# Two rings for the second plain tile of the output projections

## The chip, the cores and the metric

The kernel runs on one core of a Trainium2 chip. The metric is the device time of one execution in microseconds; the median of three runs of the kernel before is 1833.44 us. Several engines work side by side and each takes its own instructions in a fixed order: PE (TensorE, matrix products), DVE (VectorE), ACT (ScalarE), POOL (GpSimd, here mostly an issuer of transfers) and SP (SyncE, the issuer of all weight loads).

## The reference, cut to what matters

One step of a two-layer encoder over 640 tokens (512 of a prompt, 128 samples) with 2048 channels. The last step of each layer is the output projection, and only this step is touched:

```
y_a = c * silu(a_gate)                     # convolution group
y_b = o_b * silu(b_gate)                   # window attention group
y_c = mem_attention(cq, mem_k, mem_v) * silu(c_gate)
y = concatenate([y_a, y_b, y_c], axis=-1) @ w_out
return x + y, new_conv, new_k, new_v
```

## The kernel before, in words

Activations stand with channels on partitions: `R` holds 16 tiles of 128 channels by 640 tokens. A float32 product is made of three products of a high and a low half: each operand is split into a rounded copy (`split`, an ACT copy on L138) and the remainder (a DVE subtraction on L139). `HL` holds the split activations, high halves first. A weight tile of 128 output channels comes as four parts of 128x512; each part is loaded by SP (L149), split by ACT and DVE, and read by 24 products of 128x320 on PE (four blocks of 128 rows, three passes, two halves of the tokens).

Two sets of buffers hold such weights. The ring of the input projection lies in the pool `wp`: `wr` for the load, `wh` and `wl` for the halves, three buffers each; `wprep` uses it. The ring of the output projection lies in the pool `sw`: `sr` (six buffers for loads), `sh` and `sl` (two each); `s_prep` uses it. `sr` tiles may have 768 columns.

An output projection (from L1069 on) has 16 output tiles. Tiles j=0 and j=1 are "plain": 96 products each, L760, with the sum going to a `z` tile of PSUM; L1115 then adds the residual (`zt`) and writes `R`. The other tiles go in pairs through `s_pair`, a seven-product scheme of the Strassen kind on the middle and last channels: `combos` first makes differences of tiles of `R` (L789, eight per layer, some in place) and splits them into `th`/`tl` (three combinations, two pieces each) and back into `HL` (one combination, two pieces). `th`/`tl` live in the pool `tt`, which is opened on the same side of memory as `wp`, after `wp` is closed: of the three combinations the third (`th4`, `tl4`) lies over `wh` and `wl`, the first `tl` over `wr`. A tile waits for the last reader of what lies under it.

The first pair begins with a product `X` (18 products, weights `p1`, first loads of the pair), then `plain(True)`: 18 products with the part `a12` as loaded, then 18 with `a12 - s2` (a DVE subtraction of 128x768, L789, followed by its own split). The difference `s2` comes from `s1 = a21 + a22` (L843), which needs the third load of the pair's four.

In layer 1, L1074 first stores six tiles of `R` to memory (`y12d`, 960 KB, by POOL); the in-place differences of `combos` wait until it has landed.

The order within an engine is set by a scheduler when the program is built, from the order in the code and from priorities; weight loads and splits are of high priority. `sh_8724` and the like are names with their buffer number.

Of the kernel before, what the change touches and what calls it, by code (L numbers as in the profile page):

```python
# [58 lines left out]
def build(nc, tc, ctx, A):  # L59
# [15 lines left out]
    def open_pool(n, side):  # L75
        uid[0] += 1
        held_pools[n] = tc.tile_pool(name=f"{n}{uid[0]}", bufs=1, reuse_waits="tile", side=side)
        cur[n] = held_pools[n].__enter__()

    def close_pool(n):  # L80
        held_pools.pop(n).__exit__(None, None, None)
# [9 lines left out]
    def zt():  # L91
        return tl([P, TOK], "zt", 2)
# [16 lines left out]
    def pz():  # L109
        return tl([P, 2, 512], "z", 2, F32, zp)  # L110
# [22 lines left out]
    def half(t):  # L133
        return t.rearrange("p (s n) -> p s n", s=2)
# [114 lines left out]
    def add_sq(k, first, acc, tmp=w25):  # L249
        if first:  # L250
            ac.activation(acc, R[:, k, :], AF.Square)
        else:
            sq = tmp()
            ac.activation(sq, R[:, k, :], AF.Square)
            ve.tensor_tensor(out=acc, in0=acc, in1=sq, op=ALU.add)
# [495 lines left out]
    def proj(wsrc, prep=wprep):  # L751
        ps = pz()
        for pc in range(4):
            wh, wl = prep(wsrc[pc])
            for kk in range(4):
                k = pc * 4 + kk
                ws = slice(kk * P, (kk + 1) * P)
                for n, (w, lo) in enumerate(((wh, 0), (wh, 1), (wl, 0))):
                    for s in range(2):
                        pe.matmul(  # L760
                            ps[:, s, :HT], w[:, ws], HL[:, lo * NK + k, s * HT:(s + 1) * HT],
                            start=k == 0 and n == 0, stop=k == NK - 1 and n == 2,
                        )
        return ps
# [29 lines left out]
    def combos():  # L794
        T = {}
        tt = [
            (tl([P, 6, HT], f"th{n}", 1, F32R, cur["tt"]), tl([P, 6, HT], f"tl{n}", 1, F32R, cur["tt"]))
            for n in (2, 3, 4)
        ]
        T[2], T[3], T[4] = tt  # L800
        T[1] = hl(KA, TB)
        gs = [(slice(KA.start + g, KA.start + g + 3), slice(KB.start + g, KB.start + g + 3)) for g in (0, 3)]
        for a, b in gs:
            sub(R[:, a, TA], R[:, a, TB], R[:, a, TA])
            sub(R[:, a, TB], R[:, b, TB], R[:, a, TB])
            sub(R[:, b, TB], R[:, b, TB], R[:, a, TA])
        place = {1: (0, TA), 2: (1, TB), 3: (0, TB), 4: (1, TA)}
        for n in (3, 2, 4, 1):
            for g, ab in enumerate(gs):
                i, cs = place[n]  # L810
                if n == 4:
                    sub(R[:, ab[1], TA], R[:, ab[1], TA], R[:, ab[1], TB])
                ks = slice(3 * g, 3 * g + 3)
                split(R[:, ab[i], cs], None, T[n][0][:, ks, :], T[n][1][:, ks, :])
        return T
# [90 lines left out]
    for l in range(L):  # L906
# [35 lines left out]
        for n, (kind, i) in enumerate(ZT):  # L942
            if l == 0 and n in (8, 9):
                o, i_ = (("o_kold", "ck"), ("o_vold", "cv"))[n - 8]
                with tc.issue_after(late):
                    gp.dma_start(A[o], A[i_][:, :, ST:, :])
            ps = proj(A["w_in"][l, n])
            if n == 0:
                rstd_row(rstd, acc, 1.0 / D)
# [158 lines left out]
        for j in list(range(2)) + list(range(2, done, 2)):  # L1108
            if j < 2:
                res = zt()  # L1110
                gp.dma_start(res, resid[j])
                ps = proj(
                    [A["w_out"][l, j][:, c * 512:(c + 1) * 512] for c in range(4)], s_prep if j else wprep
                )
                ve.tensor_tensor(out=half(R[:, j, :]), in0=ps[:, :, :HT], in1=half(res), op=ALU.add)  # L1115
            else:
                s_pair(l, j, T, resid, turn if j + 2 == done else None)
            if j == 0:
                close_pool("wp")
                open_pool("tt", "right")  # L1120
            if j == 1:
                T = combos()
            for i in range(j, j + 1 if j < 2 else j + 2):
                if l == 0:
                    gp.dma_start(x1d[i], R[:, i, :])
                add_sq(i, i == 0, acc)
# [173 lines left out]
```

## Time and profile before

| what | value |
|---|---|
| runs | 1833.44, 1833.44, 1834.79 us |
| the profiled execution's own time | 1833.57 us |
| its span, first to last instruction | 1831.8 us |
| PE busy (12580 products) | 1803.6 us, 98% of the span |
| DVE, ACT, POOL busy | 1258.1, 785.0, 174.0 us |
| mean granted PE clock | 0.996 |
| output projection of layer 0, plain tiles | from about 739 to 774 us |
| output projection of layer 1, plain tiles | from about 1591 to 1628 us |

The span is 1.8 us shorter than the execution's own time; both are of the same execution. PE is busy nearly throughout, so time is to be looked for where PE stood still: in the views of waits and in the timeline around the two places in the table. In a row of the timeline the first number is the start in us from the span's start, the second how long the merged instructions took, then engine, line, operation, tiles, their number, and in brackets the idle time of the engine before it with what ended it.

### The profile page before, as it was taken

The page shows a single profiled execution, that of the slowest core. Times are in us where ns is not written, and L with a number is a line of the kernel's source. Part 1 is how long each engine was busy: PE and PEld are TensorE (multiplying, and loading weights), DVE is VectorE, ACT ScalarE, POOL GpSimd, SP SyncE. Part 2 cuts the span into 40 slices and gives each one's busy share as a digit, 9 for nine tenths or more (in the row PEclk, how much of TensorE's full clock was granted, in tenths as well). Part 3 has the DMA queues.
Part 4 walks back from the last instruction along what each step waited for, and adds up shares of the span by engine and source line. Part 5 has one row for each costly group of instructions (what it writes and reads, how often), then busy time and mean ns, then how long its engine had stood idle before and what let it go on. Part 6 is the DMA issues. An engine that isn't in the chain of part 4 may idle for free.

```text
span 1831.8 us, 32312 instructions
## 1 busy us (share of the span) xinstructions
PE 1803.6 (98%) x12580; PEld 1766.5 (96%) x12580; DVE 1258.1 (69%) x2562; ACT 785.0 (43%) x1593; POOL 174.0 (9%) x383
## 2 busy tenths in 40 slices
PE   8999999999999999999999999999999999999996
PEld 7899999999999999999999999999999999989996
DVE  7959999567555445966686999766655544776765
ACT  7831224556644334533352222555755333533331
POOL 1121210000001010100030010000001110010000
PEclk9999999999999999999999999999999999999998
DMA  8844442222222343533333332222222244442233
GB/s 283 290 129 103 105 130 76 70 64 70 87 78 84 98 162 116 171 134 116 109 102 89 82 81 78 78 67 73 73 84 85 74 139 132 158 160 84 71 113 121
DMA packets 89193, 202.30 MB, mean 110 GB/s; under 512 B 12064, under 2 KB 17104, under 8 KB 89008
## 3 DMA queue, kind: packets, MB, share of 16 engines
q1 hardware_dynamic: 68848, 139.75, 25.3%
q0 software_dynamic: 17728, 57.60, 10.3%
q10 hardware_dynamic: 2464, 2.88, 0.5%
q8 instruction: 99, 1.62, 0.4%
q14 instruction: 54, 0.44, 0.1%
HBM read 184.84 MB, written 20.33 MB: 112 GB/s over the span
## 4 chain that ended last, share of the span: by engine, by line
PE 94%; DVE 3%; DMA 2%; issue 1%; ACT 0%; SPq 0%; DVEq 0%; ACTq 0%; POOLq 0%
PE z L760 59%; PE a L821 9%; PE z L821 9%; PE a L278 2%; PE z L301 2%; PE a L497 2%; PE a L540 2%; PE a L477 2%; PE z L1145 1%; DVE R L1178 1%; PE a L528 1%; DMA wr<-w_in 1%; PE a L647 1%; PE a L673 1%; PE a L686 1%
## 5 line engine op out<-in xcount | busy, mean ns | idle before, releaser
L760 PE MATMUL z<-HL,wh 128*128 128x320 f32 x4992 | 979.5, 312 | 0.0
L760 PEld LDWEIGHTS z<-HL,wh 128*128 128x128 f32 x4992 | 788.9, 188 | 7.9 <-issue 5.3
L760 PE MATMUL z<-HL,wl 128*128 128x320 f32 x2496 | 580.4, 311 | 0.7 <-DVE wl L139 0.7
L760 PEld LDWEIGHTS z<-HL,wl 128*128 128x128 f32 x2496 | 419.3, 188 | 2.0 <-DVE wl L139 1.0
L138 ACT ACTIVATE wh<-wr 128x512 fp32r<-128x512 f32 x316 | 198.7, 629 | 448.6 <-PE z L760 373.1
L139 DVE TENSOR_TENSOR wl<-wr,wh 128x512 fp32r<-128x512 f32 x316 | 218.0, 690 | 172.7 <-ACT wh L138 163.6
L425 DVE SCALAR_TENSOR_TENSOR R<-R,sm 128x128 f32<-128x128 f32 (+1 forms) x480 | 235.4, 552 | 0.1
L138 ACT ACTIVATE sh<-sr 128x768 fp32r<-128x768 f32 (+1 forms) x125 | 98.3, 787 | 206.2 <-PE a L821 91.4
L821 PE MATMUL z<-HL,sh 128*128 128x320 f32 x728 | 160.9, 309 | 1.9 <-ACT sh L138 1.9
L139 DVE TENSOR_TENSOR sl<-sr,sh 128x768 fp32r<-128x768 f32 (+1 forms) x125 | 110.1, 881 | 40.7 <-ACT sh L138 40.5
L821 PEld LDWEIGHTS z<-HL,sh 128*128 128x128 f32 x728 | 121.7, 188 | 2.4 <-ACT sh L138 2.4
L821 PE MATMUL z<-HL,sl 128*128 128x320 f32 x364 | 113.4, 312 | 0.9 <-DVE sl L139 0.7
L139 DVE TENSOR_TENSOR g<-a,g 128x512 fp32r<-128x512 f32 x80 | 49.5, 634 | 39.8 <-ACT g L138 39.2
L821 PE MATMUL a<-th,sh 128*128 128x320 f32 x234 | 72.2, 308 | 0.0
L821 PE MATMUL a<-tl,sh 128*128 128x320 f32 x234 | 72.2, 308 | 0.0
L821 PE MATMUL a<-th,sl 128*128 128x320 f32 x234 | 72.2, 308 | 0.0
L821 PEld LDWEIGHTS z<-HL,sl 128*128 128x128 f32 x364 | 68.3, 188 | 3.2 <-DVE sl L139 3.2
L821 PE MATMUL a<-HL,sh 128*128 128x320 f32 x312 | 68.9, 308 | 0.0
L138 ACT ACTIVATE g<-a 128x512 fp32r<-128x512 f32 x80 | 42.1, 551 | 53.1 <-PE a L531 29.9
L501 DVE CUSTOM_DVE_ANT_0 g<-a,R 128x256 f32<-128x256 f32 (+1 forms) x128 | 46.4, 388 | 23.4 <-PE a L497 20.0
L513 ACT ACTIVATE g<-g,sml 128x256 f32<-128x256 f32 (+1 forms) x128 | 59.8, 468 | 0.0
L485 POOL DMA_DIRECT2D R<-brep x32 | 17.3, 541 | 407.3 <-issue 238.2
(263 smaller groups left out, 2536.0 us busy)
## 6 DMA issues: line engine op xcount, KB each, us to landing
wr<-w_in SPq DMA_DIRECT2D x304, 256.0 KB, 2.7
sr<-w_out SPq DMA_DIRECT2D x52, 384.0 KB, 3.3
sr<-w_out SPq DMA_DIRECT2D x34, 256.0 KB, 2.6
u<-w_mv SPq DMA_DIRECT2D x16, 512.0 KB, 4.0
u<-cmkT POOLq DMA_DIRECT2D x16, 512.0 KB, 3.6
u<-cmv POOLq DMA_DIRECT2D x16, 512.0 KB, 4.3
u<-w_mk SPq DMA_DIRECT2D x14, 512.0 KB, 5.1
R<-xT SPq DMA_DIRECT2D x16, 320.0 KB, 4.7
```

What stands on the lines that cost most here:

```text
L138: a = ac.activation(hi, raw, AF.Copy)
L139: v = ve.tensor_tensor(out=lo, in0=raw, in1=hi.bitcast(F32), op=ALU.subtract)
L278: pe.matmul(ps[ct][:, :256], w[:, ws], mslot(l, k, lo), start=k == 0 and n == 0, stop=k == NK - 1 and n == 2,)
L301: pe.matmul(psv[:, m, :], mslot(l, k, lo)[:, ms], w, start=k == 0 and n == 0, stop=k == NK - 1 and n == 2,)
L425: ve.scalar_tensor_tensor(out=o, in0=x, scalar=w, in1=o, op0=ALU.mult, op1=ALU.add)
L477: pe.matmul(ps[:, :HT], w[:, ws], x[:, k, :], start=n == 0, stop=n == 11)
L497: pe.matmul(ps[:, j, c0:256], q[:, p * P:(p + 1) * P], kk[n][h][:, (p - 1) * P + c0:(p + 1) * P], start=n == 0, stop=n == 1,)
L501: ve.tensor_tensor_reduce(out=x[:, j, c0:], in0=ps[:, j, c0:], in1=bt[:, c0:], scale=1.0, scalar=-3.0e38, op0=ALU.add, op1=ALU.max, accum_ ...
L513: ac.activation(x, x, AF.Exp, bias=ng[:, p:p + 1], accum_out=sm_[:, p:p + 1])
L540: pe.matmul(po[:, os], V[h][:, v, :], p[:, ms], start=v == 0 and n == 0, stop=v == 3 and n == 1, skip_group_check=True,)
L760: pe.matmul(ps[:, s, :HT], w[:, ws], HL[:, lo * NK + k, s * HT:(s + 1) * HT], start=k == 0 and n == 0, stop=k == NK - 1 and n == 2,)
L821: pe.matmul(out, a[:, k * P:(k + 1) * P], b[:, k, :], start=start and k == 0 and i == 0, stop=stop and k == n - 1 and i == 2, skip_group_c ...
```

## The change

In both layers the second plain tile (j=1) takes the first two of its four weight parts through the input projection's ring (`wprep`) and the last two through the output projection's (`s_prep`); before, all four went through the latter. `wp` is therefore closed, and `tt` opened in its place, after tile j=1 and no longer after tile j=0.

```
     def proj(wsrc, prep=wprep):
         ps = pz()
         for pc in range(4):
-            wh, wl = prep(wsrc[pc])
+            wh, wl = (prep[pc] if isinstance(prep, list) else prep)(wsrc[pc])
...
                 ps = proj(
-                    [A["w_out"][l, j][:, c * 512:(c + 1) * 512] for c in range(4)], s_prep if j else wprep
+                    [A["w_out"][l, j][:, c * 512:(c + 1) * 512] for c in range(4)], [wprep, wprep, s_prep, s_prep] if j else wprep
                 )
...
-            if j == 0:
+            if j == 1:
                 close_pool("wp")
                 open_pool("tt", "right")
-            if j == 1:
                 T = combos()
```

How this moves instructions shows best on DVE. In layer 0, around the residual sum of tile 0 (`L1115 ... z_8530`), this stood before; `sl_8724` and `sl_8754` are the low halves of the third and fourth weight part of tile 1, `tl` are the combinations:

```order
L1115 TENSOR_TENSOR R<-z_8530,zt_8528 128x640
L789 TENSOR_TENSOR R<-R 128x3x320
L139 TENSOR_TENSOR tl_1362_8785<-R,th_1361_8784 128x960 x2
L139 TENSOR_TENSOR tl_1360_8783<-R,th_1359_8782 128x960
L139 TENSOR_TENSOR tl_1364_8787<-R,th_1363_8786 128x960
L139 TENSOR_TENSOR tl_1360_8783<-R,th_1359_8782 128x960
L139 TENSOR_TENSOR sl_8724<-sr_8721,sh_8723 128x512
L139 TENSOR_TENSOR tl_1364_8787<-R,th_1363_8786 128x960
L139 TENSOR_TENSOR sl_8754<-sr_8751,sh_8753 128x512
L843 TENSOR_TENSOR sr_8832<-sr_8822,sr_8824 128x768
```

And this stands there now, up to the residual sum; `wl_8660` and `wl_8690` are the first and second part of tile 1, `sl_8720` and `sl_8750` the third and fourth:

```order
L139 TENSOR_TENSOR wl_8660<-wr_8657,wh_8659 128x512
L789 TENSOR_TENSOR R<-R 128x3x320
L139 TENSOR_TENSOR sl_8720<-sr_8717,sh_8719 128x512
L139 TENSOR_TENSOR sl_8750<-sr_8747,sh_8749 128x512
L139 TENSOR_TENSOR HL<-R,HL 128x640
L139 TENSOR_TENSOR wl_8690<-wr_8687,wh_8689 128x512
L843 TENSOR_TENSOR sr_8832<-sr_8822,sr_8824 128x768
L789 TENSOR_TENSOR R<-R 128x3x320
L789 TENSOR_TENSOR sr_8833<-sr_8832,sr_8820 128x768
L789 TENSOR_TENSOR sr_8822<-sr_8820,sr_8822 128x768
L789 TENSOR_TENSOR R<-R 128x3x320
L1115 TENSOR_TENSOR R<-z_8530,zt_8528 128x640
```

All four splits of tile 1's weights and the three operations on the pair's weights now stand ahead of the residual sum; two differences and all six `tl` follow it in one piece.

A little later on DVE, from the first split of the pair (`sl_8829`, weights of `X`) to that of the subtracted part (`sl_8881`), this stood before in layer 0 (`sr_8826` is `a12`, `w` the running sum of squares, `z_8660` the sum of tile 1):

```order
L139 TENSOR_TENSOR sl_8829<-sr_8820,sh_8828 128x768
L139 TENSOR_TENSOR HL<-R,HL 128x3x320
L1115 TENSOR_TENSOR R<-z_8660,zt_8658 128x640
L139 TENSOR_TENSOR sl_8858<-sr_8826,sh_8857 128x768
L139 TENSOR_TENSOR HL<-R,HL 128x3x320
L789 TENSOR_TENSOR sr_8826<-sr_8826,sr_8833 128x768
L255 TENSOR_TENSOR w_1329_8527<-w_1329_8527,w_1365_8813 128x640
L827 TENSOR_TENSOR R<-a_8818,R 128x320
L139 TENSOR_TENSOR sl_8881<-sr_8826,sh_8880 128x768
```

and this stands there now, in layer 0 and with other numbers in layer 1:

```order
L139 TENSOR_TENSOR sl_8829<-sr_8820,sh_8828 128x768
L1115 TENSOR_TENSOR R<-z_8656,zt_8654 128x640
L139 TENSOR_TENSOR HL<-R,HL 128x3x320
L139 TENSOR_TENSOR sl_8858<-sr_8826,sh_8857 128x768
L139 TENSOR_TENSOR HL<-R,HL 128x3x320
L255 TENSOR_TENSOR w_1329_8527<-w_1329_8527,w_1365_8813 128x640
L827 TENSOR_TENSOR R<-a_8818,R 128x320
L789 TENSOR_TENSOR sr_8826<-sr_8826,sr_8833 128x768
L139 TENSOR_TENSOR sl_8881<-sr_8826,sh_8880 128x768
```

The residual sum of tile 1 has moved ahead of a split into `HL`, and the subtraction from `a12` has moved behind L255 and L827. In layer 1 the subtraction stood behind these two before as well.

SP's queue (layer 0) now has `wr_8657`, `wr_8687`, `sr_8717`, `sr_8747` where it had `sr_8661`, `sr_8691`, `sr_8721`, `sr_8751`, then the pair's four loads as before. The first row below is the last load of tile 0:

```order
L149 DMA wr_8621<-w_out 128x512
L149 DMA wr_8657<-w_out 128x512
L149 DMA wr_8687<-w_out 128x512
L149 DMA sr_8717<-w_out 128x512
L149 DMA sr_8747<-w_out 128x512
L149 DMA sr_8820<-w_out 128x768
L149 DMA sr_8822<-w_out 128x768
L149 DMA sr_8824<-w_out 128x768
L149 DMA sr_8826<-w_out 128x768
```

The two `wr` loads wait for buffers of a ring of three that tile 0 still uses, and the six `sr` loads are issued behind them.

More of the change, by code (lines that the diff above doesn't have):

```diff
@@ L753, in proj @@
         for pc in range(4):
-            wh, wl = prep(wsrc[pc])
+            wh, wl = (prep[pc] if isinstance(prep, list) else prep)(wsrc[pc])
             for kk in range(4):
@@ L1112, in build @@
                 ps = proj(
-                    [A["w_out"][l, j][:, c * 512:(c + 1) * 512] for c in range(4)], s_prep if j else wprep
+                    [A["w_out"][l, j][:, c * 512:(c + 1) * 512] for c in range(4)], [wprep, wprep, s_prep, s_prep] if j else wprep
                 )
@@ L1117, in build @@
                 s_pair(l, j, T, resid, turn if j + 2 == done else None)
-            if j == 0:
+            if j == 1:
                 close_pool("wp")
                 open_pool("tt", "right")
-            if j == 1:
                 T = combos()
```

## The prediction

> **What bounds the kernel now.** I read the page first, then PE's waits in the two stretches where the plain tiles of the output projection run, then the timeline there, and last the transfers.
>
> ```profile
> span 1831.8 us, 32312 instructions
> PE 1803.6 (98%) x12580; PEld 1766.5 (96%) x12580; DVE 1258.1 (69%) x2562; ACT 785.0 (43%) x1593; POOL 174.0 (9%) x383
> PE 94%; DVE 3%; DMA 2%; issue 1%; ACT 0%; SPq 0%; DVEq 0%; ACTq 0%; POOLq 0%
> ```
>
> PE is busy for 98% of the span and the chain that ended last is PE for 94%. The change leaves the number and size of the products alone, so it can only move time at which PE stands still near the plain tiles. These are PE's waits there, first all of layer 0 (720 to 800 us), then all of layer 1 (1580 to 1660 us); the three numbers are the total, the times, the longest:
>
> ```profile
> PE z L760 <- DVE sl L139: 1.4, 1, 1.4
> ...
> PE z L760 <- DVE sl L139: 2.3, 1, 2.3
> PE z L821 <- ACT sh L138: 1.4, 1, 1.4
> PE z L821 <- DVE sl L139: 0.7, 2, 0.4
> ```
>
> Each layer loses once inside a plain tile (L760, a low weight half that came late), and layer 1 loses again in the first pair (L821). Together this is some 6 us; no way of ordering this stretch can win more than that, 0.3% of the time. The timeline shows the first loss, in layer 0 and in layer 1:
>
> ```profile
> 761.53 5.42 DVE L139 TENSOR_TENSOR tl<-R,th 128x960 fp32r<-128x960 f32 x5
> 765.51 0.75 PE L760 MATMUL z<-HL,sh 128*128 128x320 f32 x4
> 766.87 0.68 DVE L139 TENSOR_TENSOR sl<-sr,sh 128x512 fp32r<-128x512 f32 x1
> 767.61 0.57 PE L760 MATMUL z<-HL,sl 128*128 128x320 f32 x2 [1.35 <-DVE sl L139]
> ...
> 1618.23 0.75 PE L760 MATMUL z<-HL,sh 128*128 128x320 f32 x4
> 1621.31 0.56 PE L760 MATMUL z<-HL,sl 128*128 128x320 f32 x2 [2.33 <-DVE sl L139]
> ```
>
> Five splits of the combinations (`tl`) hold DVE for 5.4 us, and the split of tile 1's third weight part stands behind them. PE has done its four products with the high half and waits.
>
> The second place is what I call the tail: from PE's first product of the pair (`a<-HL,sh`) to the first low product with the subtracted part (`z<-HL,sl`), 38 products later. First layer 0, then layer 1:
>
> ```profile
> 773.30 0.75 PE L760 MATMUL z<-HL,sh 128*128 128x320 f32 x4
> 774.09 0.85 ACT L138 ACTIVATE sh<-sr 128x768 fp32r<-128x768 f32 x1 [1.34 <-PE z L760]
> 774.18 0.46 PE L821 MATMUL a<-HL,sh 128*128 128x320 f32 x2
> 774.38 0.82 DVE L1115 TENSOR_TENSOR R<-z,zt 128x640 f32<-128x640 f32 x1 [0.44 <-PE z L760]
> ...
> 780.07 0.41 PE L821 MATMUL z<-HL,sl 128*128 128x320 f32 x1
> ...
> 1627.87 0.46 PE L821 MATMUL a<-HL,sh 128*128 128x320 f32 x2
> 1629.52 0.82 DVE L1115 TENSOR_TENSOR R<-z,zt 128x640 f32<-128x640 f32 x1
> 1630.25 0.95 DVE L139 TENSOR_TENSOR sl<-sr,sh 128x768 fp32r<-128x768 f32 x1
> 1631.12 1.16 DVE L139 TENSOR_TENSOR HL<-R,HL 128x960 fp32r<-128x960 f32 x1
> 1632.19 0.49 DVE L827 TENSOR_TENSOR R<-a,R 128x320 f32<-128x320 f32 x1
> 1632.59 0.82 DVE L255 TENSOR_TENSOR w<-w,w 128x640 f32<-128x640 f32 x1
> 1633.32 0.96 DVE L789 TENSOR_TENSOR sr<-sr,sr 128x768 f32<-128x768 f32 x1
> 1634.39 1.36 ACT L138 ACTIVATE sh<-sr 128x768 fp32r<-128x768 f32 x2 [3.28 <-DVE sr L789]
> 1635.27 1.56 DVE L139 TENSOR_TENSOR sl<-sr,sh 128x768 fp32r<-128x768 f32 x2 [0.99 <-ACT sh L138]
> 1636.28 0.42 PE L821 MATMUL z<-HL,sl 128*128 128x320 f32 x1 [0.43 <-DVE sl L139]
> ```
>
> From 773.30 to 774.18 six products start, so one takes 0.147 us, and 38 take 5.57 us. The tail took 5.89 us in layer 0 and 8.41 us in layer 1, where the subtraction (L789) stood behind L827 and L255.
>
> **The change part by part.** *Equal work.* Four loads, eight split instructions and 96 products per tile stay, and the 256 KB of each load; cost 0.
>
> *First loss.* All four splits of tile 1 now stand ahead of the `tl`, so no `tl` can hold them up. The losses by starts are 767.61 - 765.51 - 4 x 0.147 = 1.51 us and 1621.31 - 1618.23 - 4 x 0.147 = 2.49 us. I take both away: -4.00 us.
>
> *Tail.* Late next is the tail. The new DVE order is the residual sum (L1115), a split into `HL`, a weight split, a split into `HL`, L255, L827, the subtraction. L1115 waits for tile 1's last product: it starts 0.20 us after the pair's first product (774.38 - 774.18). From the starts in layer 1's rows: L1115 0.73, `HL` 1.07, weight split 0.87, `HL` 1.07, L255 0.73, L827 0.40, together 4.87; subtraction to ACT's copy 1.07, copy to DVE's split 0.88, split to PE 1.01. Sum 0.20 + 4.87 + 2.96 = 8.03 us, against 5.57 us of products: the cover is gone in layer 0. The tail grows by 8.03 - 5.89 = 2.14 us there; layer 0 is left at -1.51 + 2.14 = +0.63 us. A PE wait inside the tail (the first two products of `plain` now stand ahead of the low products of `X` and wait for an ACT copy) is no extra: DVE sets the end.
>
> *Layer 1's DVE.* The same tail holds only if DVE has finished what stands ahead of L1115 of tile 1. That begins with the split of tile 1's second part, held by the ring: its high half can be copied when PE has read the third part of tile 0.
>
> ```profile
> L138 ACT ACTIVATE wh<-wr 128x512 fp32r<-128x512 f32 x316 | 198.7, 629 | 448.6 <-PE z L760 373.1
> ...
> 1601.59 0.69 DVE L139 TENSOR_TENSOR wl<-wr,wh 128x512 fp32r<-128x512 f32 x1
> ...
> 1611.63 0.46 PE L760 MATMUL z<-HL,wl 128*128 128x320 f32 x2
> ...
> 1617.36 2.22 DVE L139 TENSOR_TENSOR tl<-R,th 128x960 fp32r<-128x960 f32 x2
> ```
>
> Tile 0's last product started at 1611.63 + 0.15 = 1611.78; five products of tile 1 no longer stand ahead of it (-0.73), and the last reader of the buffer lies 26 products earlier (-3.82): 1607.23. ACT copies 0.35 us after such a reader (774.09, the last of the four from 773.30 starting at 773.74), so the split starts at 1607.23 + 0.35 + 0.63 = 1608.2. Behind it: this split 0.61, three operations on the pair's weights at 0.87, L1115 of tile 0 0.73, six differences and six `tl` at 1.07 (the two `tl` of 1617.36 take 2.22, overlapping 0.08 each with the next), the split of `p1` 0.87: 17.7 us, to 1625.9. The pair's first product would be at 1627.87 - 2.49 = 1625.38, L1115 could start at 1625.58. DVE is 0.3 us late. Layer 1 is then -2.49 + (8.03 + 0.3 - 8.41) = -2.57 us, if the loads are in time.
>
> *Loads.* L843 stands third in that DVE row and needs the pair's third load by 1608.8; DVE takes its instructions in order, so everything behind waits with it. Before, no load of this stretch waited for `wr`; now the pair's loads are issued behind the `wr` load that waits for the split of 1601.59. In the new order a difference and an `HL` split (1.07 + 0.74) have moved from between L734 and this split to ahead of L734, so it ends near 1600.5, and six loads follow.
>
> ```profile
> wr<-w_in SPq DMA_DIRECT2D x304, 256.0 KB, 2.7
> ...
> 1592.00:1598.00 6.00, 6.00 (x43) 6.00 (x43) 5.60 (x10) 4.86 (x8) 0.00 (x0) 1.00 0.77 253
> ...
> 1604.64 0.82 POOL L1074 DMA_DIRECT2D y12d<-R  x1 [0.80 <-DVE R L1061]
> ...
> L834 POOL DMA_DIRECT2D R<-x1d x1: 536/536/536, 1627.3 to 1627.3; - x1
> DMA to landing us min/median/max: 5.5/5.5/5.5
> ...
> L149 SPq DMA_DIRECT2D sr<-w_out x1: 328/328/328, 1628.6 to 1628.6; - x1
> DMA to landing us min/median/max: 4.9/4.9/4.9
> ```
>
> The burst of 1592 moved 253 GB/s at 0.77 of the engines' time (last two numbers): 329 KB per us when full. The `wr` load lands near 1600.6 + 2.7 = 1603.3; two loads of 256 KB, three of 384 KB and a residual load of 320 KB ahead of the store: 1984 KB or 6.0 us more, 1609.3. So L843 is late by d = 0.5 us if transfers go in the order of issue. For that speaks the SP load of 1628.6: it landed at 1633.5, after a POOL load issued 1.3 us earlier (1632.8). If the store `y12d` of 960 KB instead shares the engines, both land only after 2944 KB, 8.9 us, at 1612.2: d = 3.4. The ends are 0 and 3.4; I take 0.5, nearest to the row of 1628.6.
>
> The Trainium skill, page "DMA: Bandwidth & Descriptors", section "Queues, rings and completion order", says that each DMA engine goes round the queues that have work, packet by packet. By that rule d would be near 3.4; the order of landing above does not bear it out, though two transfers in one place prove little.
>
> *Other queues.* POOL's loads of residuals for later pairs wait for the last `tl` and their sums come a pair later: 0. In layer 0 no store competes, and two differences fewer stand in the 17.7 us stretch (2.1 us), so that DVE has 2.1 - 0.3 = 1.8 us to spare there: 0.
>
> *Sum.* Layer 0 +0.63, layer 1 -2.57 + 0.5: -1.4 us. The profiled execution took 1833.57 us, 0.13 above the median of 1833.44; from the median I forecast 1832.0 us.
>
> **The rivals.**
> 1. *The store and the loads share (slower).* Layer 1, L843: +0.63 - 2.57 + 3.4 = +1.5, 1834.9 us. It decides from d = 1.9 on: above that the change loses. For it: 960 KB now fall into the stretch of the loads. Against it: the order of landing. This is the skill's rule above.
> 2. *The tail stays short.* If L255 and L827 cost nothing because something else is later, the tails stay at 5.89 and 8.41 and the whole 4.00 us are won: 1829.4 us. Against it: layer 1 has that order already and has its long tail.
> 3. *The ring starves tile 1 (the change doesn't do what it says).* Its second part waits for its load as well as for its buffer. The load lands near 1603.3, the buffer is free at 1607.6: 4 us of cover, the same spacing in layer 0. Were the cover gone and 2 us more lost per layer, the time would be 1832.0 + 4 = 1836.0 us.
>
> **How the numbers follow.** 0.2% is 3.7 us, about what a measurement of this kernel can tell from no change. Forecast 0.68, rival 1 0.16, rival 2 0.10, rival 3 0.06. Forecast and rival 1 lie within 0.2%; rival 2 lies at its edge (4.0 us), half of it counted as faster, with a little for errors of the forecast: faster 0.06. Slower by 0.2% needs d above 5.6 or most of rival 3: 0.05. Range: from the sum with d = 0 and 0.5 us less per tail (-1.94 - 1.0 = 1830.5) up to rival 1 with 0.3 us of spare (1835.2). The forecast's own range is 1830.5 to 1833.4.
>
> **What would show it.** Right: no PE wait on `z<-HL,sl` of L760 in either layer; a tail of about 8.0 us in layer 0, with a PE wait on ACT `sh` at L821 that was not there; about 8.3 to 9 us in layer 1; L843 waiting for a transfer in layer 1, 0.5 us or so. Wrong: L843 held for 2 us and more; a wait of L760 on `wh` or `wl`; or a tail in layer 0 still below 7 us.

## The result, and the profile after

The changed kernel takes 1840.9 us (five runs, 1839.8 to 1842.5) against 1833.4 us (five runs, 1833.3 to 1834.8): a ratio of 1.0038, 95% interval 1.0027 to 1.0050. It is 7 us slower. The profiled execution took 1839.8 us, and its span is 6.2 us longer than the one before. The head of its page:

```profile
span 1838.0 us, 32318 instructions
PE 1808.3 (98%) x12580; PEld 1770.3 (96%) x12580; DVE 1257.8 (68%) x2562; ACT 786.7 (43%) x1593; POOL 174.2 (9%) x383
PE 91%; DVE 4%; DMA 3%; issue 1%; ACT 0%; SPq 0%; DVEq 0%; ACTq 0%; POOLq 0%
```

The chain that ended last now has 3% less PE in it, and 1% each more DVE and transfers. PE's waits, first around layer 0's plain tiles, then around layer 1's (total, times, longest):

```profile
PE z L821 <- ACT sh L138: 2.9, 3, 1.4
PE z L821 <- DVE sl L139: 0.6, 2, 0.4
...
PE a L821 <- DVE sl L139: 3.3, 1, 3.3
PE z L821 <- ACT sh L138: 1.1, 2, 0.7
PE z L821 <- DVE sl L139: 0.2, 1, 0.2
```

The waits inside the plain tile (L760) are gone in both layers, as the change meant it. More than they cost is lost in the first pair (L821). The timeline of DVE and PE there, layer 0 and then layer 1:

```profile
758.37 0.96 DVE L843 TENSOR_TENSOR sr<-sr,sr 128x768 f32<-128x768 f32 x1 [2.33 <-DMA sr<-w_out]
772.24 0.46 PE L821 MATMUL a<-HL,sh 128*128 128x320 f32 x2
773.39 0.82 DVE L1115 TENSOR_TENSOR R<-z,zt 128x640 f32<-128x640 f32 x1
781.21 0.41 PE L821 MATMUL z<-HL,sl 128*128 128x320 f32 x1 [0.43 <-DVE sl L139]
788.52 0.56 PE L821 MATMUL z<-HL,sh 128*128 128x320 f32 x2 [1.17 <-ACT sh L138]
789.25 0.42 PE L821 MATMUL z<-HL,sl 128*128 128x320 f32 x1 [0.17 <-DVE sl L139]
...
1616.07 0.96 DVE L843 TENSOR_TENSOR sr<-sr,sr 128x768 f32<-128x768 f32 x1 [3.83 <-DMA sr<-w_out]
1628.28 0.46 PE L821 MATMUL a<-HL,sh 128*128 128x320 f32 x2
1633.23 0.81 DVE L1115 TENSOR_TENSOR R<-z,zt 128x640 f32<-128x640 f32 x1
1633.37 0.64 PE L821 MATMUL a<-HL,sl 128*128 128x320 f32 x1 [3.32 <-DVE sl L139]
1641.40 0.41 PE L821 MATMUL z<-HL,sl 128*128 128x320 f32 x1
```

DVE stands still at L843 in both layers, for 2.33 and 3.83 us, waiting for the pair's third weight load. What follows on DVE is late by that much, less what it had to spare. The third place is 788.52, where PE waits for the weights of the second tile of the pair. The rows of the chain of waits that name a load (issue, time to landing) are these three:

```profile
749.75 8.49 DMA sr<-w_out
...
781.19 6.55 DMA sr<-w_out
...
1606.23 9.72 DMA sr<-w_out
```

The first and the last are the loads that L843 waits for, the second feeds the wait at 788.52. Three windows of the trace after close the reading: in each layer from the landing of the `wr` load that waited for the ring to the landing of L843's load, then the stretch behind the wait of 3.3 us. The numbers are the length, the busy time of PE, its weight loads, DVE, ACT and POOL, then granted clock, share of the transfer engines, GB/s:

```profile
750.50:758.20 7.70, 7.70 (x55) 7.70 (x54) 5.43 (x8) 3.12 (x5) 0.54 (x1) 1.00 0.92 325
1606.60:1615.90 9.30, 9.30 (x65) 9.30 (x65) 4.37 (x6) 2.42 (x4) 0.75 (x2) 1.00 0.98 335
...
1633.00:1640.00 7.00, 6.63 (x26) 6.64 (x27) 6.14 (x8) 1.23 (x2) 4.51 (x9) 0.53 0.89 282
```

While those loads are under way, the transfer engines are over 90% busy. In the 7 us behind the wait of 3.3 us PE was granted 0.53 of its clock on average.

### The profile page after: what moved, and what is told of

Same layout as the page of the kernel before. It is cut to its first block, busy times and chain, and to the rows that moved or that the text cites. A ratio compares the mean times of both kernels' runs of the same rounds, so it can differ in the third digit from the quotient of the medians.

```text
span 1838.0 us, 32318 instructions
## 1 busy us (share of the span) xinstructions
PE 1808.3 (98%) x12580; PEld 1770.3 (96%) x12580; DVE 1257.8 (68%) x2562; ACT 786.7 (43%) x1593; POOL 174.2 (9%) x383
## 3 DMA queue, kind: packets, MB, share of 16 engines
q8 instruction: 99, 1.62, 0.4%
## 4 chain that ended last, share of the span: by engine, by line
PE 91%; DVE 4%; DMA 3%; issue 1%; ACT 0%; SPq 0%; DVEq 0%; ACTq 0%; POOLq 0%
PE z L760 57%; PE a L821 9%; PE z L821 8%; PE a L278 3%; PE z L301 2%; DMA sr<-w_out 2%; PE a L497 2%; PE a L540 2%; PE a L477 2%; PE z L1144 1%; DVE R L1177 1%; PE a L528 1%; DMA wr<-w_in 1%; PE a L647 1%; DVE HL L139 1%
## 5 line engine op out<-in xcount | busy, mean ns | idle before, releaser
L760 PE MATMUL z<-HL,wh 128*128 128x320 f32 x5056 | 991.6, 312 | 0.0
L760 PEld LDWEIGHTS z<-HL,wh 128*128 128x128 f32 x5056 | 799.0, 188 | 7.9 <-issue 5.3
L760 PE MATMUL z<-HL,wl 128*128 128x320 f32 x2528 | 587.9, 311 | 0.5 <-DVE wl L139 0.5
L760 PEld LDWEIGHTS z<-HL,wl 128*128 128x128 f32 x2528 | 424.9, 188 | 1.8 <-DVE wl L139 0.8
L821 PE MATMUL z<-HL,sh 128*128 128x320 f32 x728 | 161.9, 310 | 4.6 <-ACT sh L138 4.6
L821 PEld LDWEIGHTS z<-HL,sh 128*128 128x128 f32 x728 | 122.1, 189 | 6.1 <-ACT sh L138 6.1
L821 PE MATMUL z<-HL,sl 128*128 128x320 f32 x364 | 114.0, 314 | 0.8 <-DVE sl L139 0.8
L821 PEld LDWEIGHTS z<-HL,sl 128*128 128x128 f32 x364 | 68.7, 189 | 3.7 <-DVE sl L139 3.7
L821 PE MATMUL a<-tl,sh 128*128 128x320 f32 x234 | 72.2, 308 | 0.0
L821 PE MATMUL a<-th,sl 128*128 128x320 f32 x234 | 72.2, 308 | 0.0
L821 PE MATMUL a<-th,sh 128*128 128x320 f32 x234 | 72.2, 308 | 0.0
L821 PE MATMUL a<-HL,sh 128*128 128x320 f32 x312 | 70.4, 314 | 0.0
```

The source lines that it names most:

```text
L760: pe.matmul(ps[:, s, :HT], w[:, ws], HL[:, lo * NK + k, s * HT:(s + 1) * HT], start=k == 0 and n == 0, stop=k == NK - 1 and n == 2,)
L821: pe.matmul(out, a[:, k * P:(k + 1) * P], b[:, k, :], start=start and k == 0 and i == 0, stop=stop and k == n - 1 and i == 2, skip_group_c ...
```

## The experiments

My theory was that late loads hold DVE at L843, and that a bunch of residual loads delays the weights of the pair's second tile. The rivals were the order on DVE alone, the store alone, and the low clock as a cost of its own. Ratios are to the kernel before, measured beside each group; 0.001 is 1.8 us.

| run | ratio (95%) | | run | ratio (95%) |
|---|---|---|---|---|
| layer0_only | 1.0013 (1.0004 to 1.0022) | | loads_sub_resid | 0.9989 (0.9981 to 0.9998) |
| layer1_only | 1.0015 (1.0006 to 1.0024) | | filled | 1.0045 (1.0031 to 1.0059) |
| small_store | 1.0032 (1.0019 to 1.0044) | | tl_later | 1.0013 (1.0004 to 1.0021) |
| sub_first | 1.0027 (1.0017 to 1.0038) | | before_reordered | 0.9993 (0.9984 to 1.0002) |
| sums_late | 1.0011 (1.0003 to 1.0020) | | all_four | 0.9983 (0.9975 to 0.9992) |
| loads_first | 1.0017 (1.0008 to 1.0025) | | all_five | 0.9959 (0.9947 to 0.9972) |
| resid_held | 1.0024 (1.0013 to 1.0036) | | before_five | 0.9967 (0.9955 to 0.9979) |
| loads_resid | 0.9993 (0.9985 to 1.0002) | | | |

**One layer at a time.**

```
- [wprep, wprep, s_prep, s_prep] if j else wprep
+ ([wprep, wprep, s_prep, s_prep] if l == 0 else s_prep) if j else wprep     # layer0_only; l == 1: layer1_only
```

> The change in layer 0 alone; layer 1 is that of the kernel before. Theory (two causes, one per layer): in layer 0 the order on DVE makes the tail long and POOL's residual loads, which now leave in one bunch, delay the weights of the pair's second tile; in the trace of the changed kernel PE has lost 2.9 us by the start of layer 1's output projection, so this kernel takes 1833.4 + 2.9 = 1836.3 us. Rival (the loss is the transfers of layer 1 and the low clock behind them, and what layer 0 loses is given back): 1833.4 us or less.

> The change in layer 1 alone; layer 0 is that of the kernel before. Theory: PE waits 3.3 us for the low half of the first product of the pair and then runs some 6 us at about half the clock; the trace of the changed kernel loses 6.1 - 2.9 = 3.2 us in this layer, so 1833.4 + 3.2 = 1836.6 us, and the granted clock shows the dip here too. Rival (the dip comes from what happened in layer 0, or the layers do not add): no dip, 1834.5 us or less.

Measured: +2.4 and +2.8 us. Each layer loses by itself, about equally, and together they give 5.2 of the 7 us, whose interval is 5 to 9. The eleven runs of layer0_only lie far apart, 1835.0 to 1840.1 us, and the profiled one is near their upper end. The half clock is not tied to a place: layer1_only has it behind the same wait of 3.32 us, in layer0_only the untouched layer 1 had it behind the old wait in tile 1 (2.74 us, below), and the kernel before had that wait, 2.33 us at 1621.31, without it.

```profile
1628.74 0.63 PE L760 MATMUL z<-HL,sl 128*128 128x320 f32 x1 [2.74 <-DVE sl L139]
```

**The store.**

```
+ if l == L - 1: gp.dma_start(y12d, R[:, KA, TB])     # the whole store, at the start of the layer's input projection
...
- gp.dma_start(y12d, R[:, KA, TB])
+ gp.dma_start(y12d[:, :, HT - 32:], R[:, KA, TOK - 32:TOK])
```

> The changed kernel with the store of layer 1 (y12d) cut to 32 of its 320 columns at its place; the whole store is made once at the start of layer 1's input projection, where it holds old values, so the last two output tiles are computed from wrong values. The order on all engines is otherwise that of the changed kernel. Theory (store and loads share the transfer engines): the third load of the pair lands some 2.5 us earlier or more, L843 waits 1.5 us at most instead of 3.8, PE's wait of 3.3 us shrinks below 1.5 us and the dip of the clock with it: 1840.9 - 1.8 - 2.3 = 1836.8 us, at best 1840.9 - 5.6 = 1835.3. Rival (the order on DVE alone makes layer 1 late): L843 and PE wait as before the cut, 1840.5 us or more.

Its timeline, layer 1:

```profile
1618.88 0.96 DVE L843 TENSOR_TENSOR sr<-sr,sr 128x768 f32<-128x768 f32 x1 [2.02 <-DMA sr<-w_out]
...
1636.19 0.63 PE L821 MATMUL a<-HL,sl 128*128 128x320 f32 x1 [2.41 <-DVE sl L139]
```

The expected gain did not come. With a tenth of the store L843 still waits 2.02 us. In the six profiles that have the change in layer 1, the whole store and the same order of loads, it waits 2.45 to 4.45 us, so by this wait the store's share lies between 0.4 and 2.4 us. The measure is loose: late loads can also hold DVE one step earlier (in the profile of `filled`, a run further down, it waited 2.64 us at 1613.49 for ACT's copy of an earlier load). PE's wait for the pair's first low half fell from 3.3 to 2.4 us. The loads alone do the rest: layer 0, where no store runs, has waits of 2.33 to 2.81 us in its seven profiles with the change.

**The subtraction first.**

```
+ with tc.issue_after(cut_):           # cut_: the subtraction from a12
+     add_to(R[:, j1, TA], X)          # L827; then the splits into HL, then L255
```

> The changed kernel, but in the first pair of each layer the subtraction from a12 (L789) and its split stand ahead of the second split into HL, of L255 and of L827, as nearly as in the kernel before. Theory: in layer 0 the two waits of the tail (1.42 + 0.43 us) go, and the weights of the second tile are issued 2 to 3 us earlier, so their waits (1.17 + 0.17) go as well; layer 1 gains 0.5 us, its 3.3 us wait and the dip stay: 1840.9 - 3.2 - 0.5 = 1837.2 us. Rival (order on DVE is all there is, in both layers): layer 1's wait goes too, 1834 us or less. Rival (residual loads alone, not the order): the waits at the second tile stay, 1838.6 us or more.

1.0027 against 1.0038: some 2 us where 3.7 were expected, and the intervals overlap. L843 waited as before (4.45 us in layer 1), so the splits at the pair's start stayed late, and the second tile still waited 1.47 us at 790.16. The order of the tail was not the main cause.

**The sums behind the tl; the loads ahead of the ring's.**

```
+ with tc.issue_after(last["tl"]):     # sums_late: fourth tl
      L843 and the two L789 on the pair's weights
```
```
  SP: wr (part 0), sr, sr, a11, a21, a22, a12, wr (part 1)      # loads_first; the change has wr, wr, sr, sr, a11, ...
```

> The changed kernel, but the three operations on the pair's weights (L843 and two L789) stand behind the fourth tl on DVE, no longer ahead of the residual sum of tile 0. Transfers are as in the changed kernel. Theory (the three loads of the pair come late in both layers, and L843, moved early, holds DVE 2.3 to 2.8 us in layer 0 and 3.0 to 4.5 us in layer 1, so that the first splits of the pair are late; the clock then falls to about half for some us after the gaps): L843 waits for nothing, the first product with a low half in the pair waits under 0.5 us in both layers, no stretch at half clock follows there; what is left is the wait at the second tile of layer 0. Before + 2 us, a ratio of 1.000 to 1.002. Rival (DVE has too much work there in any order): the same 5 us and more over before, 1.003.

> The changed kernel, but on SP's queue the loads of tile 1's last two parts and the pair's four loads stand ahead of tile 1's second load, which waits for the ring. The loads then leave where those of the kernel before left (near 740 and 1593 us). Theory (the loads that queue behind the ring's load are the cause): L843 waits for no transfer in either layer, though it stands early on DVE; the wait on the low half at the start of the pair goes, and the stretches at half clock with it. Before + 2 us or less, ratio 0.999 to 1.002; left are the tail's wait on ACT and the wait at the second tile. Rival (the store alone delays L843 in layer 1): L843 in layer 1 still waits 2 us, 1.003. Rival (order on DVE): waits stay as they are, 1.003.

L843 in sums_late (L846 there), then in loads_first, layer 0 and layer 1 each:

```profile
766.82 0.95 DVE L846 TENSOR_TENSOR sr<-sr,sr 128x768 f32<-128x768 f32 x1
1625.36 0.96 DVE L846 TENSOR_TENSOR sr<-sr,sr 128x768 f32<-128x768 f32 x1
...
752.52 0.96 DVE L843 TENSOR_TENSOR sr<-sr,sr 128x768 f32<-128x768 f32 x1 [0.94 <-DMA sr<-w_out]
1608.88 0.96 DVE L843 TENSOR_TENSOR sr<-sr,sr 128x768 f32<-128x768 f32 x1 [0.83 <-DMA sr<-w_out]
```

One edit moves the waiting instruction, the other the loads, and both win 4 to 5 us. That shows the cause of the larger half: an instruction that stands early on DVE and loads that land late. Details missed: in sums_late PE still waited 1.62 us for the pair's first low half in layer 1, since three operations now stood in the row that is short of time; in loads_first L843 still waits 0.8 to 0.9 us, earlier, where DVE has time.

**The residual loads.**

```
+ gp.tensor_copy(R[:, j, :1], a11[:, :1])      # POOL, ahead of each residual load of a later pair
  gp.dma_start(R[:, j, :], resid[j])
```

> The changed kernel, but POOL loads the residuals of each later pair only when that pair's first weights have landed (a copy of one column by POOL stands ahead of each load), no longer all in one bunch. Theory: the weight load for the pair's second tile no longer lands behind 8 to 10 residual loads, it takes under 3 us where it took 6.5, and PE's wait at the second tile of layer 0 (1.2 to 2.0 us) goes, with the half clock behind it where there was one (1.4 us); L843's waits and the tail stay. 2 to 3 us less than the changed kernel, ratio to before about 1.0015 to 1.002. Rival (that load is late because it is issued late): the wait at the second tile stays, 1.003 or more.

The SP loads of the second tile's place, here issued at 781.7 and 782.3 (time to landing, shortest, median, longest):

```profile
L149 SPq DMA_DIRECT2D sr<-w_out x2: 328/328/328, 781.7 to 782.3; - x2
DMA to landing us min/median/max: 2.6/3.2/3.8
```

The first load takes 2.6 us where it took 6.55, and PE's wait there is gone. The ratio fell from 1.0038 to 1.0024, 2.6 us. The intervals overlap, so the cause is shown by the wait that went. Its size is known roughly: 2.6 us here, 4.4 us between loads_first (1.0017) and the next run (0.9993), which differ by this edit alone, and 1.8 + 1.1 = 2.9 us in the ledger below.

**Both, and nothing else.**

> The changed kernel with the two edits that touch transfers alone: the pair's loads ahead of tile 1's second load on SP, and the residual loads held. No order on DVE is set by hand. Theory (the prediction left out two things and nothing else: L843 held by late loads, and the weights of the second tile behind the residual loads): what is left is the prediction's own sum, before - 1.4 us, with up to 1.5 us of half clock on top, a ratio of 0.999 to 1.0003. Rival (a third cause, on DVE): 1.0008 or more.

0.9993: the prediction had 1832.0 / 1833.44 = 0.9992, so a third cause as large as these two is not needed. PE's waits that are left, in layer 0 and layer 1:

```profile
PE z L821 <- ACT sh L138: 1.1, 1, 1.1
PE a L821 <- DVE sl L139: 0.7, 1, 0.7
...
PE z L821 <- ACT sh L138: 1.8, 2, 1.4
PE z L821 <- DVE sl L139: 0.4, 1, 0.4
```

The sum does not come true term by term, though. Its profile (L843 is L849 there, L1115 is L1137), layer 0 and then layer 1:

```profile
753.91 0.96 DVE L849 TENSOR_TENSOR sr<-sr,sr 128x768 f32<-128x768 f32 x1 [2.23 <-DMA sr<-w_out]
772.67 0.56 PE L821 MATMUL a<-HL,sh 128*128 128x320 f32 x2
773.85 0.82 DVE L1137 TENSOR_TENSOR R<-z,zt 128x640 f32<-128x640 f32 x1
782.23 0.34 PE L821 MATMUL z<-HL,sl 128*128 128x320 f32 x1
...
1636.30 0.41 PE L821 MATMUL z<-HL,sl 128*128 128x320 f32 x1 [0.43 <-DVE sl L139]
```

L843 still waits 2.23 us in layer 0 and 1.45 us in layer 1, but 4 us and more earlier than in the changed kernel. The first loss of layer 0 is won as summed (772.67 against 774.18). Its tail takes 9.56 us, not 8.03: the residual sum starts 1.18 us behind the pair's first product, not 0.20, and the split of `X`'s weights now stands behind it. Layer 1 goes from 2.16 us late at 782.23 to 0.02 late at 1636.30, 2.1 us won where 2.1 to 2.6 were summed. So this profile is 0.2 us shorter than that of the kernel before, not 1.4; that the median meets the forecast so closely is in part luck, and its interval is -2.8 to +0.4 us.

**The gap filled.**

```
+ for _ in range(20):     # layer 1, first pair, behind the first two products
+     m = pe.matmul(fill, w[0][:, :P], x[0][:, 0, :], start=True, stop=True, ...)
```

> The changed kernel, but in layer 1 PE does 20 products more right behind the first two of the pair, into a sum that nobody reads (2.9 us of the 3.3 us in which it waited there). Everything else keeps its order. Theory (after a gap PE runs at about half clock for some us, whatever caused the gap): the remaining wait is 0.4 to 0.8 us, no half clock follows in layer 1, and the time is 1.4 to 2.6 us below that of the changed kernel, a ratio to before of 1.0022 to 1.003. Rival (the low clock comes from the load on the transfer engines or on DVE at that place, not from the gap): the half clock stays, ratio 1.0035 or more.

```profile
1629.64 3.10 PE L823 MATMUL a<-HL,sh 128*128 128x320 f32 x20
1634.76 0.41 PE L825 MATMUL a<-HL,sl 128*128 128x320 f32 x1 [1.72 <-DVE sl L139]
1641.45 0.56 PE L825 MATMUL z<-HL,sh 128*128 128x320 f32 x2 [1.41 <-ACT sh L138]
...
1634.00:1641.00 7.00, 5.22 (x32) 4.70 (x32) 6.44 (x8) 1.18 (x2) 4.74 (x10) 1.00 0.87 270
```

The clock stayed at 1.00, as expected of a clock that falls behind gaps, yet the 1.4 to 2.6 us expected were not won (1.0045). Where PE had run at half clock it now waits again, 1.41 us for the subtracted part: DVE sets the end of the tail, and the slow products lay in its shadow. I had counted the half clock as 2.3 us of this layer's loss; this run refutes that.

**A version that beats both.** loads_sub_resid joins three edits; the others also place the fourth combination and the splits into HL by hand.

```
+ held.append(partial(sub, ...)); held.append(partial(split, ...))     # n == 4 and n == 1 in combos
+ with tc.issue_after(cut_):    # cut_: the subtracted part's split; all_five: n == 1 and L255 behind the next split
+     for f in held: f()
```

> The three edits together on top of the change: loads first on SP, the subtraction from a12 ahead of the second split into HL, L255 and L827, and the residual loads held. Theory: PE waits under 0.5 us in all at the places named in both layers; the losses of the kernel before (1.4 us in layer 0, 2.3 + 1.4 + 0.4 us in layer 1) go too: before - 3.5 us, ratio 0.998. Rival (something else is late next by about as much): 0.9995 to 1.001.

> The changed kernel with another order on DVE alone, its transfers untouched: the fourth combination (two L789, two tl), the splits into HL, L255 and L827 stand behind the split of the subtracted part; the splits of the pair's weights come 4.3 us earlier. Theory (DVE has 2.3 to 4.5 us too little there, and only there): L843 still waits 2 to 4 us, but PE's waits in the pair shrink to 0 to 1 us in layer 0 and 0 to 1.5 us in layer 1, and the half clock there is rare: before - 1 us, ratio 0.999 to 1.0005; left is the wait at the second tile of layer 0. Rival (late loads bound PE in any order): 1.002 or more.

> The kernel before, without the change, with the same order on DVE and with the residual loads held back until the pair's first weights have landed. Theory: four tl instead of five and six stand ahead of the splits of tile 1, so the wait of 1.4 us in layer 0 and of 2.3 us in layer 1 shrinks to 0.3 and 1.3 us, and the tail's waits go: ratio 0.998 to 0.999. Rival (the two rings are needed to win the first loss): 1.000.

> The change with all edits: the pair's loads first on SP, the residual loads held, and the order on DVE of the run with the later tl. Theory: L843 waits under 3 us and that is covered, PE waits under 0.5 us in either layer at the plain tiles and the first pair: before - 5 us, ratio 0.997 to 0.998. Rival (late loads or DVE still late): 0.9985 or more.

> The run with all edits, but the splits into HL and L255 stand behind the split of the next weights (those of the pair's first tile from the last 512 channels), where PE waited 1.64 us in both layers. Theory: those waits go, with the half clock that followed some of them: 3 us below the run with all edits, ratio to before 0.9965 to 0.9975. Rival (the next split, of the second tile, is then late by as much): 0.998 or more.

> The same order on DVE and the same held residual loads on the kernel before, without the change and without the loads first. Theory (the two rings are worth little once DVE's order is right; the wait inside tile 1 was 0.0 in layer 0 and 0.5 us in layer 1 in the run with the earlier order): ratio 0.997 to 0.9985, at most 1 us behind the run with the change. Rival (the rings are needed): 0.999 or more.

Four of these missed at first for one reason: behind the pieces moved out of the way stood the next weight split. In all_four:

```profile
781.45 0.82 DVE L256 TENSOR_TENSOR w<-w,w 128x640 f32<-128x640 f32 x1
782.18 0.69 DVE L140 TENSOR_TENSOR sl<-sr,sh 128x512 fp32r<-128x512 f32 x1
...
782.93 0.42 PE L826 MATMUL z<-HL,sl 128*128 128x320 f32 x1 [1.64 <-DVE sl L140]
```

The same 1.64 us show in tl_later and before_reordered. In loads_sub_resid the subtracted part's own split stood behind the splits into HL, and in layer 1 the pair's first low half was still 1.4 us late. tl_later, whose residual loads are bunched, lost more in the next product of layer 0, where L843 (L848 there) of the second pair waited for its load:

```profile
798.22 0.96 DVE L848 TENSOR_TENSOR sr<-sr,sr 128x768 f32<-128x768 f32 x1 [3.32 <-DMA sr<-w_out]
...
801.37 0.41 PE L826 MATMUL a<-HL,sl 128*128 128x320 f32 x1 [1.11 <-DVE sl L140]
```

all_five moves the pieces one split further, and PE's waits in layer 0 and in layer 1 are then

```profile
PE a L826 <- ACT sh L139: 0.5, 1, 0.5
...
PE a L826 <- ACT sh L139: 0.5, 1, 0.5
```

It takes 1827.8 us beside 1834.7 for the kernel before, a ratio of 0.9959. The same order without the change, before_five, takes 1828.3 us (0.9967) with one wait of 0.6 us left in layer 1's tile 1 beside the two of 0.5. The intervals overlap: once DVE's order is right, these runs cannot tell whether the change and the loads first are worth anything. The 6.9 us that all_five wins (5.1 to 9.7) are about all that the prediction allowed to any order here, some 6 us.

## Why the prediction was wrong, point by point

It said 1832.0 us with at most 1835.2; it was 1840.9. The steps that failed are the terms that it put at 0.5 us (the loads of layer 1) and at nothing (the loads of layer 0, the other queues). The same products in both traces give the ledger (after minus before):

- *First loss: right.* The wait at L760 went in both layers; layer 1's pair starts at 1628.28 against 1627.87, 0.41 late, where it came with 3.0 from layer 0 (L726 on DVE at 1595.03 against 1592.02): 2.6 us won, and 2.49 were summed.
- *Tail: right by itself.* From L1115 to the first product with the subtracted part I had 7.83 us; it took 781.21 - 773.39 = 7.82 in layer 0 and 8.17 in layer 1. Rival 2 is out. That this tail is now set by DVE is what let every delay on DVE through.
- *"In layer 0 ... 1.8 us to spare there: 0": failed.* L843 waited 2.33 us there too, which I had not worked out for this layer at all. L1115 started 1.15 us behind the pair's first product instead of 0.20: +0.95 us.
- *"late by d = 0.5 us if transfers go in the order of issue": failed, and it is the largest term.* L843 waited 3.83 us, above both my ends (0 and 3.4), and L1115 came 4.95 us behind the first product instead of 1.0. Two things went wrong. The store did not stay behind the loads: the sum that releases it (L1061) stands earlier in the new order, and POOL issued it before SP issued the third load at 1606.23; I had taken its time from the old order.

```profile
1605.98 0.83 POOL L1074 DMA_DIRECT2D y12d<-R  x1 [0.95 <-DVE R L1061]
```

  And a load does not have the engines to itself until the next one's turn: in layer 0, where no store runs, 1984 KB or 2.0 MB had been issued up to that load, but 7.7 us at 325 GB/s moved 2.5 MB before its last byte landed. The two transfers issued after it, SP's fourth load (750.4, 9.0 us) and POOL's second `zt` (751.9, 7.2 us), landed only 1 us behind it. In layer 1 the load landed after 9.3 us at 335 GB/s, 3.1 MB; my end of 3.4 us had 2944 KB in 8.9 us. The Trainium skill's rule that the prediction cites, page "DMA: Bandwidth & Descriptors", section "Queues, rings and completion order", made d near 3.4; this trace agrees with it better than with the order that I took from one row. Rival 1 had the place and nearly the d of layer 1 (3.4 against a wait of 3.83), but loads that share are enough, without a store.
- *"Other queues ... 0": failed.* The residual loads come a pair before they are needed. In the kernel before they left in threes from 766.18 to 778.49; now eleven of them leave between 771.83 and 781.05, just ahead of SP's load for the second tile at 781.19. It cost 2.92 - 1.14 = 1.78 us in layer 0, by these rows of before and those of after at 781.21 and 789.25 (780.07 stands in the prediction):

```profile
786.33 0.31 PE L821 MATMUL z<-HL,sl 128*128 128x320 f32 x1
```

- *Layer 1's second tile:* from 5.12 us late at 1641.40 to 6.2 at the end, 1.1 us, of the same kind (SP's load of 1641.37 took 5.75 us); the prediction left it out.
- *Rival 3* did not happen: no wait on `wh` or `wl` at L760.
- *The clock* was not in the sum. In layer 1 it was covered. Whether it is what makes the runs of the changed kernel differ by 2.6 us among themselves was not tried, and their mean clocks do not show it: 0.995 in the slowest, 0.994 in the others.

The sum: forecast -1.4 in the two layers, -0.4 at the pair's start in layer 0 (0.3 of it stood there before the plain tiles began: an `HL` split of 737.22 is at 736.90 after), +0.95 and +1.78 in layer 0, +4.3 in layer 1's tail (3.33 of it L843's wait beyond 0.5), +1.1 behind it: +6.3, against 6.2 in the spans. loads_resid, which makes the failed terms small, gives a time that fits the rest of the sum within its interval; layer 0's tail does not fit, by 1.5 us.

## What to carry to other kernels

When an edit puts a load that must wait for a buffer into a queue, everything issued behind it leaves in one bunch; work out when the bunch as a whole has landed, and use that for each load in it. When it moves an instruction that waits for a load ahead of others on an in-order engine, its wait is everyone's wait; first ask whether it could stand where it stood. And when a list of hidden work is made, ask not only when it is needed but what it will stand in front of.

## What the runs showed of the hardware

PE's granted clock falls to one half behind short gaps, not always. Counting the waits in the two stretches over the 17 profiles: behind 3.3 us it fell 4 times of 4, behind 2.0 to 2.8 us 3 of 4, behind 1.4 to 1.8 us 8 of 20; four times more it fell behind some 1.1 us with a second wait of 0.5 to 0.7 us close by. Of these 19 stretches 16 lasted 3.4 us by the granted clock, and three, all behind 3.3 us, lasted 6.8 us. Two windows of layer0_only, in such a stretch behind a wait of 1.52 us and right after it:

```profile
792.50:795.85 3.35, 3.35 (x15) 3.35 (x14) 0.78 (x1) 0.00 (x0) 0.00 (x0) 0.50 0.76 212
795.95:799.00 3.05, 3.05 (x23) 3.05 (x22) 1.69 (x2) 0.85 (x1) 0.00 (x0) 1.00 0.07 26
```

From 792.42 to 796.01 us 14 products start where 3.59 / 0.147 = 24 would: 1.5 us, which nothing covers there. That a watch on PE's activity halves the clock over free-running windows of 3.4 us is what the Trainium skill says, page "TensorE: Matmul & The Clock Gate", section "Part 1: The HAM clock gate (the "warmup" mystery)"; the lengths of 3.4 and 6.8 us agree, but less than half such a window of idling was often enough here.
